# First loads and first projection of a two-layer diffusion backbone: unread products, latents first, half chunks by turns

## Chip, cores and metric

The kernel runs on one NeuronCore of a Trainium2 chip. The metric is the device time of one launch, in microseconds. Three runs of the kernel before took 780.47 us in the median (778.85 to 781.42).

## What is computed

Two layers work on 512 latent tokens (x) and 256 context tokens (ctx) of 1024 channels. The change lies at the start of the first one: the modulation (`_adaln`), the norm, and the projection by `w_in`.

```python
def _rmsnorm(x, g):
    xf = x.astype(jnp.float32)
    y = xf * lax.rsqrt(jnp.mean(xf * xf, axis=-1, keepdims=True) + RMS_EPS)
    return (y * g.astype(jnp.float32)).astype(x.dtype)

def _adaln(cond, w, b):
    m = jax.nn.silu(cond) @ w + b
    return jnp.split(m, 3, axis=-1)
...
        shift, scale, gate = _adaln(c, ada_w[layer], ada_b[layer])
        shift_c, scale_c, gate_c = _adaln(c_ctx, ada_w[layer], ada_b[layer])
        h_l = _rmsnorm(x, norm_g[layer]) * (1.0 + scale[:, None]) + shift[:, None]
        h_c = _rmsnorm(cx, norm_g[layer]) * (1.0 + scale_c) + shift_c
...
    z = jnp.concatenate([h_c, h_l], axis=1) @ w_in
```

Behind that stand latent attention and a bidirectional recurrence in layer 0 (whose decay uses `softplus(-lambda)`), neighbourhood attention in layer 1, a gate on each layer's output, and a last norm.

## The kernel before

Channels lie on the 128 partitions, tokens in the columns: x is eight tiles `x0` to `x7` of 128 x 768, columns 0 to 511 the latents (LAT), 512 to 767 the context (CTX). All is float32. A product of the projection is made of three float32r ones: each operand is split into a high and a low part (`hh`, `hl` for the normed block, `w0t0h`, `w0t0l` for a weight tile), and high x high, low x high and high x low are summed in PSUM. ScalarE writes the high part, VectorE the low one.

The first stage has these steps.

- **Loads**, all from the SP queue, which issues them in program order: x (L175), the modulation weights, the weight tiles `w0t` of the projection. `load_w` (L113) issues from there. At most eight loads are under way, since each uses one of eight semaphores in turn, and the issue that reuses one waits for the landing of the load that had it.
- **Norm** (`norm0`, L356): ScalarE squares each x tile into `sq`, VectorE adds the squares into `acc0`, PE sums them over partitions (L296, `pssum`), ScalarE takes a root (`r00t`, L304), VectorE turns it into a reciprocal root (`r00r`, L305 to L309), PE transposes and spreads it (`r00b`, L322), ScalarE copies it out as `rsb0` (L323). Names with r00 belong to the latents, with r01 to the context.
- **Modulation** (`ada_mm`, L215): 32 columns of PE at a time, eight blocks of the condition against a chunk of `ada_w`; the result is copied out (`rows`, L227), transposed (`psc`, L232) and reduced into shift `as` and scale `am` of one or two blocks (L234 to L250). Blocks 0 and 1 come as half chunks of 128 columns (`ada_prep1`, `ada_go1`, tensor `ada0`), the pairs (2,3), (4,5), (6,7) as the chunks 1, 2 and 3 of 256 columns with 5, 6 and 7 for the scale; blocks 2 and 3 are chunk 1, and the names `psada_2`, `psada_4`, `psada_6` give the first block.
- **Normed block** (`h_block` by `hb(j, c)`, L338 to L341): VectorE multiplies x by scale and root, ScalarE adds the shift into `hh`, VectorE the rest into `hl`.
- **Projection** (`z_t`, L141): tiles 0 and 1 (`psx0`, `psx1`) and 8 (`psg8`): 3 tiles x 8 blocks x 3 products, each for 512 latent and 256 context columns, 144 instructions. Then `lru_x` copies psx0 and psx1 out (L537, L539), and tile 2 follows in the same PSUM tile as psx0.

The order in which the instructions of one engine stand is not that of the code: the Tile framework sets it with a scheduler, by its own estimate of durations, and each engine then works through it strictly in order. `behind(PE, ACT)` and `tc.issue_after(mark)` tie instructions behind the last one that an engine has been given. The first stage is written out by hand from L416 to L460, the call of `z_t` for tile 8; the softplus of `lambda` is L501 to L515, the loads for the next stage are `prep_n(0)` and `ropen` (L899).

Of the kernel before, what the change touches and what calls it, by code (L numbers as in the profile page):

```python
# [46 lines left out]
def build(nc, tc, A, out, dbg=None):  # L47
# [5 lines left out]
    PE, ACT, DVE = mybir.EngineType.PE, mybir.EngineType.Activation, mybir.EngineType.DVE  # L53
# [45 lines left out]

    HE = (G,)  # L100
# [73 lines left out]
    def x_load(j):  # L174
        SY.dma_start(x_tiles[j], A["xin"][j])  # L175
# [180 lines left out]
    def norm0():  # L356
        sq = {}
        for j in range(8):
            sq[j] = th(f"sq{j}")
            S.activation(sq[j], x_tiles[j], AF.Square)  # L360
            if j == 4:
                S.activation(root, sq[0][:, 0:1], AF.Sqrt)
            for w in (LAT, CTX) if j == 7 else (slice(0, NT),):
                if j:
                    V.tensor_tensor(acc0[:, w], (acc0 if j > 1 else sq[0])[:, w], sq[j][:, w], ALU.add)
                if j == 7:
                    c = w is CTX
                    n, pp = (NL, NC)[c], (zz, zz3)[c]
                    ps = pp(f"pssum{c}")
                    sq_sum(ps, acc0[:, w], n, True, True)  # L370
                    if c == 0:
                        rs_bc("r00", ps, n, rsb0[:, w], pp)
                    else:
                        norm0c = lambda: rs_bc("r01", ps, n, rsb0[:, CTX], pp)
        return norm0c
# [51 lines left out]
    norm0c()
    with behind(PE, ACT):
        wt[0] = kfun(split_raw("w0t0", raw0, (8, 128)))
        hb(0, 1)  # L430
        ada_prep(1)
        ada_go1(1)
# [71 lines left out]
    V.tensor_scalar(z, e, 2.0, None, ALU.add)  # L504
    V.reciprocal(z, z)
    V.tensor_tensor(z, z, e, ALU.mult)
    V.tensor_tensor(w, z, z, ALU.mult)
    V.tensor_scalar(q, w, 1.0 / 19, None, ALU.mult)
    for d in range(17, 1, -2):
        V.scalar_tensor_tensor(q, q, 1.0 / d, w, ALU.add, ALU.mult)  # L510
    V.scalar_tensor_tensor(q, q, 1.0, z, ALU.add, ALU.mult)
    V.tensor_scalar(nl, nl, 0.0, None, ALU.max)
    V.scalar_tensor_tensor(sp4, q, 2.0, nl, ALU.mult, ALU.add)
    V.tensor_scalar(nsp4, sp4, -4.0, None, ALU.mult)
    V.tensor_scalar(sp4, sp4, 4.0, None, ALU.mult)  # L515
# [1326 lines left out]
```

## Time and profile before

| What | Value |
|---|---|
| median of three runs | 780.47 us |
| profiled execution, its own time | 780.51 us |
| its span | 778.7 us |
| PE busy | 742.4 us (95%) |
| DVE busy | 507.5 us (65%) |
| ACT busy | 415.6 us (53%) |
| POOL busy | 163.7 us (21%) |
| DMA, mean over the span | 122 GB/s |

Busy time is the union of an engine's instructions; a busy PE is not one at its peak, as the ends of its pipelined products are modelled. The chain that ended last is the work followed back from the last instruction, at each step to what released it: 75% of it is PE, 12% DVE, 5% ACT. The first 62 us, which the change rewrites, are read from the timeline, which lists an engine's instructions with start and duration.

### The profile page before, as it was taken

How to read it: one execution, taken by the hardware profiler on the slowest of the kernel's cores; microseconds unless marked ns; L12 is line 12 of the kernel's file. 1: busy time of each engine (PE TensorE's matmuls, PEld its weight loads, DVE VectorE, ACT ScalarE, POOL GpSimd, SP SyncE). 2: the span in 40 equal slices, each digit the busy share in tenths (PEclk: the TensorE clock that was granted, in tenths of full speed). 3: DMA queues.
4: the chain of work that ended last, by engine and by line, in shares of the span. 5: the costliest groups of instructions: out<-in, count | busy, mean ns of one | idle time of the engine just before them, and what ended most of it. 6: DMA issues, size and time to landing. Idle time of an engine off the chain costs nothing.

```text
span 778.7 us, 13220 instructions
## 1 busy us (share of the span) xinstructions
PE 742.4 (95%) x4966; PEld 652.8 (84%) x4966; DVE 507.5 (65%) x1051; ACT 415.6 (53%) x811; POOL 163.7 (21%) x191
## 2 busy tenths in 40 slices
PE   2999999999999999999999999999999999999995
PEld 2678898787788877888998899888888799889995
DVE  5748499887478777753396567546653766568544
ACT  5424867964467777542245355535542645456633
POOL 0000002003153477404210022002200211021414
PEclk9999999999999999999999999999999999999998
DMA  8913403411455553257021550236124541336203
GB/s 332 407 49 109 134 28 122 162 42 28 118 157 141 177 169 126 89 172 261 28 82 46 144 163 16 91 113 190 38 99 140 174 120 55 109 102 170 82 1 109
DMA packets 33598, 95.29 MB, mean 122 GB/s; under 512 B 4608, under 2 KB 6784, under 8 KB 33536
## 3 DMA queue, kind: packets, MB, share of 16 engines
q1 hardware_dynamic: 32960, 93.93, 37.5%
q8 instruction: 39, 0.64, 0.3%
q10 hardware_dynamic: 576, 0.52, 0.2%
q14 instruction: 23, 0.19, 0.1%
HBM read 73.99 MB, written 4.19 MB: 100 GB/s over the span
## 4 chain that ended last, share of the span: by engine, by line
PE 75%; DVE 12%; ACT 5%; issue 4%; DMA 3%; POOL 1%; SPq 0%; POOLq 0%; ACTq 0%; DVEq 0%
PE psg L141 11%; PE psv L1270 8%; PE psq L141 7%; PE w0oy L1175 7%; PE pskl L141 6%; PE psx L141 4%; PE w1oy L1175 4%; PE pt L1387 3%; PE pskc L141 3%; PE psada L215 2%; PE s L1346 2%; PE s L808 2%; PE s L1347 2%; PE po L1370 2%; PE po L1371 2%
## 5 line engine op out<-in xcount | busy, mean ns | idle before, releaser
L764 POOL TENSOR_SCALAR p<-p,rc 128x512 f32<-128x512 f32 (+1 forms) x96 | 77.7, 812 | 325.8 <-DVE rc L763 309.7
L1354 ACT ACTIVATE p<-s,nm 128x512 f32<-128x512 f32 x64 | 43.8, 686 | 37.0 <-DVE nm L1352 20.6
L1390 DVE TENSOR_TENSOR ptl<-pt,pth 128x512 fp32r<-128x512 f32 x64 | 43.6, 687 | 26.7 <-ACT pth L1389 26.7
L1389 ACT ACTIVATE pth<-pt 128x512 fp32r<-128x512 f32 x64 | 37.3, 595 | 34.7 <-PE pt L1387 25.5
L1352 DVE CUSTOM_DVE_ANT_1 s<-s,bias 128x512 f32<-128x512 f32 x48 | 33.2, 696 | 16.3 <-PE s L1347 14.3
L1387 PE MATMUL pt<-ident,p 128*128 128x128 f32 x256 | 40.0, 272 | 0.0
L615 POOL TENSOR_TENSOR mix<-mix,la 128x256 f32<-128x256 f32 x4 | 3.6, 905 | 172.8 <-DVE la L609 124.8
L844 DVE TENSOR_TENSOR pt<-pt,pt 128x512 fp32r<-128x512 f32 x48 | 31.9, 681 | 11.5 <-ACT pt L843 11.4
L843 ACT ACTIVATE pt<-pt 128x512 fp32r<-128x512 f32 x48 | 27.4, 595 | 16.1 <-PE pt L881 16.0
L763 DVE RECIPROCAL rc<-rs 128x1 f32<-128x1 f32 x96 | 15.2, 158 | 31.6 <-ACT p L1354 22.2
L1346 PE MATMUL s<-k,q 128*128 128x256 f32 x128 | 34.3, 292 | 0.4 <-DMA q<-qx 0.2
L812 ACT ACTIVATE p<-s,nm 128x768 f32<-128x768 f32 x32 | 28.8, 901 | 10.7 <-DVE nm L810 10.4
L1387 PEld LDWEIGHTS pt<-ident,p 128*128 128x128 f32 x256 | 31.1, 140 | 4.0 <-issue 0.4
L810 DVE TENSOR_REDUCE nm<-s 128x1 f32<-128x768 f32 x32 | 30.4, 951 | 4.6 <-PE s L808 4.1
L1347 PE MATMUL s<-k,q 128*128 128x256 f32 x128 | 33.3, 284 | 0.0
L1370 PE MATMUL po<-pth,v 128*128 128x256 f32 (+1 forms) x96 | 31.6, 335 | 0.0
L1371 PE MATMUL po<-ptl,v 128*128 128x256 f32 (+1 forms) x96 | 29.6, 324 | 0.0
L881 PE MATMUL pt<-ident,p 128*128 128x128 f32 x192 | 28.7, 273 | 0.0
L862 PE MATMUL po<-pt,v 128*128 128x256 f32 x96 | 26.1, 296 | 1.7 <-DVE pt L844 1.6
L861 PE MATMUL po<-pt,v 128*128 128x256 f32 x96 | 26.6, 294 | 0.4 <-DVE rcc L763 0.4
L1346 PEld LDWEIGHTS s<-k,q 128*128 128x128 f32 x128 | 24.3, 190 | 3.0 <-issue 1.4
L1200 ACT ACTIVATE sq<-xr 128x512 f32<-128x512 f32 (+1 forms) x16 | 8.2, 522 | 33.1 <-DVE xr L1181 27.1
(966 smaller groups left out, 2636.8 us busy)
## 6 DMA issues: line engine op xcount, KB each, us to landing
ada_0r<-ada SPq DMA_DIRECT2D x22, 512.0 KB, 5.0
ada_4r<-ada SPq DMA_DIRECT2D x22, 512.0 KB, 5.4
q<-qx SPq DMA_DIRECT2D x32, 256.0 KB, 5.0
bias<-bias SPq DMA_DIRECT2D x16, 256.0 KB, 2.7
x<-xin SPq DMA_DIRECT2D x8, 384.0 KB, 6.3
xr<-xin SPq DMA_DIRECT2D x8, 384.0 KB, 7.0
x1d<-xr SPq DMA_DIRECT2D x8, 256.0 KB, 5.2
x<-x1d SPq DMA_DIRECT2D x8, 256.0 KB, 4.2
```

The costliest lines, as they stand in the source:

```text
L141: P.matmul(ps, a(k), b[k][:, c], start=(k == 0 and i == 0), stop=(k == nk - 1 and i == 2),)
L764: G.tensor_scalar(p, p, rc, 0.5, ALU.mult, ALU.mult)
L1175: P.matmul(ps, a, b[k][:, c], start=(n == m == 0 and ps is dst[0][0] and not second), stop=(n == 7 and m == 2), skip_group_check=True,)
L1270: P.matmul(ps, tok(a[k], t), b[:, k % 4], start=(k == 0 and i == 0), stop=(k == 7 and i == 2))
L1346: P.matmul(s[:, :256], lhs, kap, start=(i == 0), stop=False, skip_group_check=True)
L1347: P.matmul(s[:, 256:], lhs, k2[:, CTX], start=False, stop=(i == 1), skip_group_check=True)
L1354: S.activation(p, s, AF.Exp, bias=nm, scale=-1.0, accum_out=rsum)
L1370: P.matmul(dst, vv, h, start=first, stop=False, skip_group_check=True)
L1371: P.matmul(dst, vv, l, start=False, stop=last, skip_group_check=True)
L1387: P.transpose(ps[:, 128 * j : 128 * j + 128], p1[hd, b][:, 128 * c : 128 * c + 128], ident)
L1389: S.activation(h, ps, AF.Copy)
L1390: V.tensor_tensor(l, ps, f(h), ALU.subtract)
```

## The change

It does six things. Forty products of a filled tile `junk` by itself go to PE at the start, into a PSUM tile that nobody reads. x is loaded in two parts, first the eight latent halves, then, behind the first modulation and weight loads, the eight context halves. The norm runs once for the latents and once for the context. Blocks 0 to 3 are modulated by half chunks, loaded by turns with the weight tiles 0, 1 and 8. The projection is written block by block over the three tiles (`xk`), the latents of blocks 0 to 3 before their context. Softplus is tied behind VectorE's last instruction of the stage, `w0n0` and `ropen` behind its last load.

```diff
+    WARM = 40
...
+    G.memset(junk[:, :512], 1.0)
...
+    idle = pa.tile([128, 512], F32, tag="a", name="idle")
+    for _ in range(WARM):
+        P.matmul(idle, junk[:, :128], junk[:, :512], start=True, stop=True)
...
-    def x_load(j):
-        SY.dma_start(x_tiles[j], A["xin"][j])
+    def x_load(j, c):
+        w = (LAT, CTX)[c]
+        SY.dma_start(x_tiles[j][:, w], A["xin"][j][:, w])
...
+    def norm0(c):
+
+        n, w = (NL, NC)[c], (LAT, CTX)[c]
         for j in range(8):
...
+            sq = sqc[:, j] if c else th(f"sq{j}")[:, :NL]
+            S.activation(sq, x_tiles[j][:, w], AF.Square)
+            if j == 0:
+                prev = sq
+            else:
+                V.tensor_tensor(acc0[:, w], prev if j == 1 else acc0[:, w], sq, ALU.add)
+            if j == 0 and c == 0:
+                S.activation(root, sq[:, 0:1], AF.Sqrt)
+        ps = (zz, paa)[c](f"pssum{c}")
+        sq_sum(ps, acc0[:, w], n, True, True)
+        bc(f"r0{c}", rs(f"r0{c}", ps, n), n, rsb0[:, w], (zz, paa)[c])
...
+    def xk(c, js):
+
+        w = (LAT, CTX)[c]
+        for j in js:
+            for ps, ft in FIRST:
+                wh, wl = wt[ft]
+                for i, (a, b) in enumerate(((wh, hh), (wl, hh), (wh, hl))):
+                    P.matmul(
+                        ps[:, w], a(j), b[j][:, w], start=(j == 0 and i == 0), stop=(j == 7 and i == 2)
+                    )
+
     for j in range(8):
...
+        x_load(j, 0)
+    for j, ft in ((0, 0), (1, 1)):
+        ada_prep1(j)
+        load0t(ft)
+    for j in range(8):
+        x_load(j, 1)
+    ada_prep1(2)
+    load0t(8)
+    ada_prep1(3)
+    norm0(0)
+    with behind(DVE):
+        split0t(0)
...
+    ada_go1(1)
     hb(1, 0)
...
+    with behind(DVE):
+        split0t(1)
+    norm0(1)
+    for j in range(2):
+        hb(j, 1)
...
+    ada_go1(2)
+    hb(2, 0)
+    with behind(DVE):
+        split0t(8)
+    xk(0, [0, 1, 2])
+    ada_go1(3)
+    hb(3, 0)
     ada_prep(2)
...
     ada_prep(6)
...
+    xk(0, [3])
+    for j in range(2, 4):
+        hb(j, 1)
+    xk(1, [0, 1, 2, 3])
     ada_prep(3)
...
     ada_prep(7)
...
+    for p in (2, 3):
+        ada_go(p)
+        for j in (2 * p, 2 * p + 1):
+            for c in range(2):
+                hb(j, c)
+        for j in (2 * p, 2 * p + 1):
+            for c in range(2):
+                xk(c, [j])
...
+    with tc.issue_after(h_mark):
+        V.tensor_scalar(z, e, 2.0, None, ALU.add)
...
+    with tc.issue_after(load_mark):
+        prep_n(0)
+        SY.dma_start(ropen, A["ropen"])
```

What the scheduler makes of it is seen at three places. **ACT, from the last square to the first block**, before:

```order
L360 ACTIVATE sq7_158<-x7_102 128x768
L304 ACTIVATE r00t_168<-pssumFalse_161,eps_104 128x4
L304 ACTIVATE r01t_238<-pssumTrue_182,eps_104 128x2
L227 ACTIVATE rows0_0_224<-psada0_0_207 128x128
L323 ACTIVATE rsb0_122<-r00b_175 128x512
L323 ACTIVATE rsb0_122<-r01b_245 128x256
L121 ACTIVATE w0t0h_249<-w0t0r_201 128x1024
L340 ACTIVATE hh0_185<-x0_95,as0_116 128x512
```

and now (`w0t0h`, `w0t1h` are the high parts of the weight tiles, `rows0_0` the modulation of block 0 copied out of PSUM):

```order
L369 ACTIVATE sq7_227<-x7_144 128x512
L123 ACTIVATE w0t0h_250<-w0t0r_180 128x1024
L311 ACTIVATE r00t_237<-pssum0_230,eps_146 128x4
L234 ACTIVATE rows0_0_287<-psada0_0_270 128x128
L330 ACTIVATE rsb0_164<-r00b_244 128x512
L234 ACTIVATE rows0_1_316<-psada0_1_299 128x128
L123 ACTIVATE w0t1h_328<-w0t1r_186 128x1024
L347 ACTIVATE hh0_254<-x0_137,as0_158 128x512
```

The splits of two weight tiles now stand ahead of the root and of hh0; the context's root has gone from here.

**PE, around the first products of the projection**, before:

```order
L322 MATMUL r01b_245<-ident_67,r01r_236 128x128 x2
L232 MATMUL psc0_0_226<-ident_67,rows0_0_224 128x128
L215 MATMUL psada0_1_260<-ada010r_203,c34_109 32x128 x8
L215 MATMUL psada0_1_260<-ada011r_205,c34_109 32x128 x8
L141 MATMUL psx0_441<-hh0_185,w0t0h_249 128x512
L141 MATMUL psx0_441<-hh0_185,w0t0h_249 128x256
L232 MATMUL psc0_1_279<-ident_67,rows0_1_277 128x128
L215 MATMUL psada0_2_300<-ada0_1_0r_256,c34_109 32x256 x4
L215 MATMUL psada0_2_300<-ada0_1_4r_258,c34_109 32x256 x4
L215 MATMUL psada0_2_300<-ada0_5_0r_292,c34_109 32x256 x4
L141 MATMUL psx0_441<-hl0_193,w0t0h_249 128x512
```

and now, from the last product of block 1 on:

```order
L434 MATMUL psx1_370<-hl1_263,w0t1h_328 128x512
L303 MATMUL pssum1_347<-ones_154,acc0_165 128x2 x2
L434 MATMUL psg8_371<-hh0_254,w0t8h_401 128x512
L329 MATMUL r01b_359<-ident_67,r01r_350 128x128 x2
L222 MATMUL psada0_2_372<-ada020r_196,c34_151 32x128 x8
L222 MATMUL psada0_2_372<-ada021r_198,c34_151 32x128 x8
L239 MATMUL psc0_2_391<-ident_67,rows0_2_389 128x128
L222 MATMUL psada0_3_432<-ada030r_202,c34_151 32x128 x8
L222 MATMUL psada0_3_432<-ada031r_204,c34_151 32x128 x8
L434 MATMUL psx0_369<-hh2_256,w0t0h_250 128x512
```

Between the latents of block 1 and those of block 2 now stand the sum over the context, a product of tile 8, the spreading of the context's root, and two blocks of modulation. Before, a chunk for two blocks stood there, with products of blocks 0 and 1 between and behind its parts.

**DVE, between the first latents and the context's sum**, now (`acc0` is the sum of the squares):

```order
L348 SCALAR_TENSOR_TENSOR hl0_262<-x0_137,as0_158,hh0_254 128x512
L373 TENSOR_TENSOR acc0_165<-sqc_166 128x256
L373 TENSOR_TENSOR acc0_165<-acc0_165,sqc_166 128x256 x2
L348 SCALAR_TENSOR_TENSOR hl1_263<-x1_138,as0_158,hh1_255 128x512
L127 TENSOR_TENSOR w0t1l_330<-w0t1r_186,w0t1h_328 128x1024
L373 TENSOR_TENSOR acc0_165<-acc0_165,sqc_166 128x256 x4
L312 TENSOR_SCALAR r01m_351<-pssum1_347 128x2
L313 RECIPROCAL r01r_350<-r01t_352 128x2
```

The context's sums, which were made before the first root, now alternate with the low parts of blocks 0 and 1 and of tile 1.

## Rows read from the trace of the kernel before

**Rows 1.** Waits of PE, 14 to 62 us: us in total, times, longest.

```profile
PE psx L141 <- ACT hh L340: 0.9, 2, 0.5
```

**Rows 2.** Windows: length, busy us of PE, PEld, DVE, ACT, POOL, PEclk, DMA share, GB/s.

```profile
20.00:40.00 20.00, 19.50 (x152) 12.11 (x154) 14.69 (x32) 9.46 (x16) 0.00 (x0) 1.00 1.03 408
```

**Rows 3.** Timeline of the DMA queue, loads in the first 30 us: start, us.

```profile
12.09 0.33 SPq L115 DMA_DIRECT2D ada_4r<-ada  x1
...
13.06 0.33 SPq L115 DMA_DIRECT2D ada_0r<-ada  x1
...
14.34 0.33 SPq L115 DMA_DIRECT2D ada_4r<-ada  x1
...
27.20 0.33 SPq L115 DMA_DIRECT2D ada_4r<-ada  x1
...
27.62 1.24 SPq L115 DMA_DIRECT2D ada_0r<-ada  x1
...
28.96 0.38 SPq L115 DMA_DIRECT2D ada_4r<-ada  x1
```

**Rows 4.** Timeline of POOL, its last fill but one.

```profile
0.91 0.33 POOL L188 MEMSET c<- 128x272 f32 x1
```

**Rows 5.** Timeline of PE: start, us, line, tiles, shapes, count.

```profile
19.13 1.12 PE L322 MATMUL r00b<-ident,r00r 128*128 128x128 f32 x4
...
20.47 0.42 PE L232 MATMUL psc<-ident,rows 128*128 128x128 f32 x1
...
23.23 1.01 PE L141 MATMUL psx<-hh,w0t0h 128*128 128x512 f32 x2 [0.48 <-ACT hh L340]
...
24.04 0.42 PE L232 MATMUL psc<-ident,rows 128*128 128x128 f32 x1
...
27.48 0.52 PE L141 MATMUL psx<-hh,w0t0l 128*128 128x512 f32 x2
...
27.93 0.64 PE L215 MATMUL psada<-ada_4r,c 128*32 128x256 f32 x8
...
28.49 0.62 PE L141 MATMUL psx<-hh,w0t0h 128*128 128x512 f32 x2
...
42.15 0.51 PE L141 MATMUL psx<-hh,w0t1l 128*128 128x512 f32 x2
...
42.50 0.28 PE L141 MATMUL psg<-hl,w0t8h 128*128 128x256 f32 x1
...
44.03 0.38 PE L232 MATMUL psc<-ident,rows 128*128 128x128 f32 x2
...
59.96 0.58 PE L141 MATMUL psx<-hh,w0t2h 128*128 128x512 f32 x2
```

**Rows 6.** Timeline of ACT, the first root, row scale and split.

```profile
17.44 0.26 ACT L304 ACTIVATE r00t<-pssumFalse,eps 128x4 f32<-128x4 f32 x1 [3.53 <-PE pssumFalse L296]
...
20.29 0.60 ACT L323 ACTIVATE rsb<-r00b 128x512 f32<-128x512 f32 x1 [0.74 <-PE r00b L322]
...
21.04 1.06 ACT L121 ACTIVATE w0t0h<-w0t0r 128x1024 fp32r<-128x1024 f32 x1
```

**Rows 7.** Timeline of DVE: softplus, r00r, x0, w0t0's low part, lx0.

```profile
4.49 1.37 DVE L510 SCALAR_TENSOR_TENSOR sp<-sp,sp 128x8 f32<-128x8 f32 x7
...
18.41 0.16 DVE L309 SCALAR_TENSOR_TENSOR r00r<-r00t,r00r 128x4 f32<-128x4 f32 x1
...
21.67 1.15 DVE L338 SCALAR_TENSOR_TENSOR x<-x,am,rsb 128x512 f32<-128x512 f32 x2
...
22.74 1.22 DVE L125 TENSOR_TENSOR w0t0l<-w0t0r,w0t0h 128x1024 fp32r<-128x1024 f32 x1
...
58.73 0.42 DVE L537 COPY lx<-psx 128x256 f32<-128x256 f32 x1 [4.46 <-PE psx L141]
```

**Rows 8.** Windows at the end of the span, columns as in rows 2.

```profile
769.00:771.00 2.00, 0.78 (x6) 0.61 (x5) 0.56 (x3) 0.68 (x2) 1.25 (x2) 1.00 0.52 179
...
771.00:773.00 2.00, 0.66 (x2) 0.29 (x2) 0.63 (x5) 0.38 (x1) 0.08 (x1) 0.50 0.19 66
```

More of the change, by code (lines that the diff above doesn't have):

```diff
@@ L52, in build @@
     V, S, P, G, SY = nc.vector, nc.scalar, nc.tensor, nc.gpsimd, nc.sync
-    PE, ACT, DVE = mybir.EngineType.PE, mybir.EngineType.Activation, mybir.EngineType.DVE
+    PE, ACT, DVE, SP = (getattr(mybir.EngineType, e) for e in ("PE", "Activation", "DVE", "SP"))
     def f(ap):
@@ L351, in build @@
     acc0 = px.tile([128, NT], F32, name="acc0")
+    sqc = px.tile([128, 8, NC], F32, name="sqc")
     root = cst.tile([128, 1], F32, name="root")
-    def norm0():
-        sq = {}
+    def norm0(c):
+        n, w = (NL, NC)[c], (LAT, CTX)[c]
         for j in range(8):
[L359 to L375, printed above, removed]
+            sq = sqc[:, j] if c else th(f"sq{j}")[:, :NL]
[9 more added lines that the diff above has]
+        bc(f"r0{c}", rs(f"r0{c}", ps, n), n, rsb0[:, w], (zz, paa)[c])
     wt = {}
@@ L414, in go, with load0t, split0t @@
         next(going[key], None)
-    psx = []
-    for j in range(8):
-        x_load(j)
-    ada_prep1(0)
-    norm0c = norm0()
+    raw = {}
+    def load0t(ft):
+        raw[ft] = load_w(f"w0t{ft}", A["w0t"][ft], (8, 128))
+    def split0t(ft):
+        wt[ft] = kfun(split_raw(f"w0t{ft}", raw[ft], (8, 128)))
+    def xk(c, js):
[7 more added lines that the diff above has]
+                    )
@@ L421, in build @@
+    for j in range(8):
+        x_load(j, 0)
[10 more added lines that the diff above has]
+        split0t(0)
     hh = [th(f"hh{j}", F32R) for j in range(8)]
     hl = [th(f"hl{j}", F32R) for j in range(8)]
-    raw0 = load_w("w0t0", A["w0t"][0], (8, 128))
-    ada_prep1(1)
     ada_go1(0)
     hb(0, 0)
[L427 to L432, printed above, removed]
@@ L433, in build @@
-    hb(1, 0)
-    hb(1, 1)
-    ada_prep(5)
+    ada_go1(1)
+    hb(1, 0)
+    with behind(DVE):
[3 more added lines that the diff above has]
+        hb(j, 1)
+    psx = [zz("psx0"), zz("psx1")]
+    psg8 = zz3("psg8")
+    FIRST = ((psx[0], 0), (psx[1], 1), (psg8, 8))
+    ada_go1(2)
[5 more added lines that the diff above has]
+    hb(3, 0)
     ada_prep(2)
-    ada_go(1)
     ada_prep(6)
-    hb(2, 0)
-    hb(2, 1)
+    xk(0, [3])
@@ L461, in build @@
+    h_mark = next(i for i in reversed(nc.cur_bb.bb.instructions) if i.engine == DVE)
+    load_mark = next(i for i in reversed(nc.cur_bb.bb.instructions) if i.engine == SP)
+    wt.clear()
     for j in range(8):
@@ L503, in build @@
     S.activation(e, e, AF.Exp)
[L504 to L515, printed above, removed]
+    with tc.issue_after(h_mark):
+        V.tensor_scalar(z, e, 2.0, None, ALU.add)
+        V.reciprocal(z, z)
+        V.tensor_tensor(z, z, e, ALU.mult)
+        V.tensor_tensor(w, z, z, ALU.mult)
+        V.tensor_scalar(q, w, 1.0 / 19, None, ALU.mult)
+        for d in range(17, 1, -2):
+            V.scalar_tensor_tensor(q, q, 1.0 / d, w, ALU.add, ALU.mult)
+        V.scalar_tensor_tensor(q, q, 1.0, z, ALU.add, ALU.mult)
+        V.tensor_scalar(nl, nl, 0.0, None, ALU.max)
+        V.scalar_tensor_tensor(sp4, q, 2.0, nl, ALU.mult, ALU.add)
+        V.tensor_scalar(nsp4, sp4, -4.0, None, ALU.mult)
+        V.tensor_scalar(sp4, sp4, 4.0, None, ALU.mult)
     dump("sp4", sp4)
```

22 lines of the change are left out of this document (1 added, 21 removed).

## Prediction

> **What bounds the kernel now.** I read the waits of TensorE first, then its timeline beside those of ScalarE, VectorE and the DMA queue, all for the first 62 us, since the change touches nothing behind them: the orders of the engines are otherwise the same, but for some twenty rows in the middle of PE and two or three of DVE that change places. PE waits only 0.9 us in all between its first product and 62 us [rows 1], so the stage looks like one bound by PE. That holds from 23.23 us on, when the first product of the projection starts; before that PE lacks data. Loads are the other limit: from 20 to 40 us the DMA engines are busy all the time, at 408 GB/s [rows 2]. The place to which I count is the start of the next projection, psx of tile 2, at 59.96 us [rows 5]. What moves it moves everything behind, because all later work hangs on these three tiles and PE goes on almost without a break.
>
> The column of the granted clock reads 1.00 in that stretch too [rows 2], but the products do not: the first 768 columns (512 and 256) take 0.81 us, from 23.23 to 24.04, and the same at 42.15 take 0.35 [rows 5]. At 27.48 they take 0.45, and the rows group behind it 0.56. So I go by durations: half speed (1.2 GHz) up to about 27.0, full (2.4 GHz) after 3.8 us of products. [...]
>
> **Loads.** The eighth issue behind a load waits for its landing, so x7 of before has landed at 13.06; 384 KB pass in 0.97 us, 512 KB in 1.28 [rows 3]. The only load with rows of 1 KB, ropen (128 KB), lies in the 1.76 us between 27.20 and 28.96, beside one of 512 KB: 0.48 at most, 0.42 by the gap to 27.62 [rows 3]. I take 0.42 for a ctx half and 0.70 for a lat half of x (256 KB, rows of 2 KB), between 0.64 by bytes alone and 0.76 as two ropen at the gap less what the longer row spares. Eight lat halves then end 8 x 0.27 = 2.2 us earlier, and w0t0, third behind them, lands at 13.06 - 2.2 + 3 x 1.28 = 14.7. Three more of 512 KB, eight ctx halves (3.4) and three (ada020, ada021, w0t8) put w0t8 at 25.8. The chunks 2 and 3 end by 38.6; none of the rest is late. By bytes alone it would be w0t0 at 14.2, w0t8 at 24.5. The Trainium skill (DMA: Bandwidth & Descriptors, Specifications) puts the smallest transfer that runs at line rate at 512 bytes, and by it the shorter rows would cost nothing and my sum would be 0.5 us smaller.
>
> **Unread products.** Forty of 512 columns start when POOL has filled junk, at some 1.3 us, behind the fills that now end at 1.24 [rows 4]. At two thirds of 0.81 for the first 3.8 us and of 0.35 after, they end near 12.7. The first sum is ready then, but its root is not taken before 15.85 (below), so they cost nothing; were that cover gone, each would cost 0.23.
>
> **First half block.** On ScalarE the split of w0t0 now stands ahead of the root r00t. It waits for the load: 14.7 + 1.06 [rows 6] + 0.1 = 15.85. From r00t to the end of r00r took 17.44 to 18.57 [rows 6, 7]; three tiny instructions slipped in, 0.1 each, make it 1.4: 17.3. The transposes r00b stand behind eight products of psada0_1, which wait for psc of block 0, and start near 17.6; with 1.12 [rows 5] and rsb 0.60 [rows 6] it is 19.3. ScalarE then has rows0_1 and the split of w0t1 (1.06) ahead of hh0: 20.85. With hh0 at two thirds of a pair, 0.73, the first product starts at 21.5 instead of 23.23, at half clock, which the trickle of products from 12.7 on cannot have kept up (16 small ones per half chunk, as little as at the end of the span).
>
> **From there to hh2, the term that decides.** In the order, r01b and the whole of block 2 stand behind one product of psg8 and behind the sum over the context, and that sum is built on VectorE between other things: hl0 0.77, three acc of 256 columns (0.38 as the third of a pair [rows 7], and 0.07 to the next that needs it) 1.35, hl1 0.77, the low part of w0t1 1.22 [rows 7], four acc 1.8. That is 5.9 us: 27.4. PE's twelve products (0.54 each for 3.8 us, then 0.23) are through by 26.5, before that sum. Then sum products 0.6, root and rsqrt 1.1, r01b 0.5 (half of r00b), rsb and x0 of the context 0.8, hh0 and hh1 of the context 0.8, rows0_2 0.25: 31.4. From psc to the first product behind it took 20.47 to 23.23, 2.76 us [rows 5], here for block 2: 34.2. w0t8 (25.8 + 1.06 = 26.9) is in time for its product, the half chunks too. So PE, with only 13 of its 144 projection products behind it, has stood idle for most of 6 us.
>
> **From hh2 to the end.** Up to psc of chunk 2 PE has 23 products of 512 columns and 36 of 256, by the full pair's 0.35 [rows 5] 5.4 + 4.2 us, four groups of psada at 0.56 [rows 5] and psc 0.4: 12.3. From that psc on, the work is what it was: 44.03 to 59.96, 15.93 us [rows 5], the wait for hh4 in it. 34.2 + 12.3 + 15.9 = 62.4, against 59.96: 2.4 us. The clock fell again while PE stood, so the first 3.8 us run at half speed and lose 1.9: 64.3. The sum is **+4.4 us**.
>
> **What costs nothing.** Softplus (18 small instructions at 0.2 [rows 7], 3.6 us) moves from under the loads to behind hl7. VectorE is idle there for 4.46 us until psx0 is done [rows 7]; without that cover it would delay the copy of psx0 and so psx of tile 2 by up to 3.6. The w0n0 and ropen loads move behind the chunks, some 2 us later than now, for work behind psx of tile 2. The eight additional squares and adds lie beside PE's waits, and are in the chain above where they are not.
>
> The profiled execution took 780.51 us with its span of 778.7, 0.04 above the median of 780.47. So 780.5 + 4.4 = **784.9 us**. A measurement here can tell about 0.3% (2.3 us) from no change.
>
> **Rivals.**
> (1) The clock stays full from the unread products on. Half of the 1.12 of r00b and a half chunk's 0.5 are saved ahead of the first product, 1.2 in all, and the 1.9 behind hh2: +1.3, 781.8. With loads by bytes alone, +0.8. [...] Against it: what the engine does at 14 to 23 now, the same small products, left it at half speed. Chance 0.25.
> (2) Each pause of PE brings half clock back, and 12 products with pauses in them never lift it: the sum products, r01b and two half chunks then take 1.3 us more ahead of hh2. That is +5.7, 786.2. The Trainium skill (TensorE: Matmul & The Clock Gate, HAM oscillation) tells of bursts of matmuls parted by waits for loads, each of which starts throttled; the fall at 771 agrees, and no row of before shows a rise broken off. Chance 0.16.
> (3) It gets faster, because PE, waiting 0.9 us in all [rows 1], is what paces the stage: an earlier first product, 20.3 at full clock, brings everything forward by 2.9 and spares the 1.9 lost between 23.23 and 27: 775.7. This needs PE fed without a break. It decides at hh2: with 12.3 + 15.9 behind it, the product of hh2 must come before 31.7 for no loss and before 29.4 for a gain that shows. Against it: with loads by bytes alone the product of w0t8 cannot come before 24.5 + 1.06, and behind that stand r01b, a half chunk, and 2.76 us. Chance 0.08.
> (4) The unread products do not do what they say: the clock stays down under them (forty at 0.54, two thirds of 0.81, to 22.9) and the first sum waits for them in PE's queue. r00t comes near 25, not 15.95: some 793. Against it, 3.8 us of products lifted the clock at 27. Chance 0.06.
>
> **Numbers.** The forecast has 0.45. Its own bounds are -1.0 (loads by bytes, a shorter step in the VectorE chain) and +1.2. Range 780.0 to 787.0: it takes in the forecast, (1) with its lower bound, and (2), and leaves out (3) and (4). Slower by over 0.3%: 0.45 + 0.16 + 0.06 and the upper edge of (1), 0.03: 0.70. Faster 0.08. The same 0.22.
>
> **What would show it.** Right: psx of tile 2 starts between 63 and 66 us, hh2's first product at 33 to 36, PE idle or in half chunks between 27 and 34, r00t behind the split of w0t0. The pair of 768 columns (or 512 alone, 0.5 against 0.23) at half speed at 21 and again at 35. VectorE's lx directly behind psx0, not behind softplus. Wrong: hh2 before 31.7, or full speed at 21 and at 35; and if psx of tile 2 is late by 4 us but the end is not, later work had slack that I don't see.

## The result and the profile after

The changed kernel takes 788.12 us (median of 4 runs, 785.01 to 789.13) against 779.78 for the kernel before (4 runs beside it). The ratio is 1.0101, 95% interval 1.0082 to 1.0119: slower, as forecast, but by 8 us instead of 4.4, and outside the range. The profiled execution took 788.36 us with a span of 786.5.

On the page of the changed kernel TensorE is busier in all, by 14.5 us, of which the unread products, from 1.46 to 12.34, are 10.9. The clock's row shows one slice of 20 us at half:

```profile
span 786.5 us, 13395 instructions
...
PE 756.9 (96%) x5038; PEld 659.0 (84%) x5038; DVE 510.4 (65%) x1061; ACT 416.1 (53%) x820; POOL 164.1 (21%) x192
...
PEclk9599999999999999999999999999999999999998
```

The windows of that stretch (columns as in [rows 2]) say how long it lasts. TensorE works 6.2 to 7.1 us of each 8, at 0.50 of full speed from 16 to 40 us; 0.51 in the third row is the last tenths behind the rise:

```profile
16.00:24.00 8.00, 6.16 (x43) 3.69 (x44) 5.74 (x20) 4.87 (x13) 0.00 (x0) 0.50 0.91 306
24.00:32.00 8.00, 6.89 (x31) 4.28 (x34) 4.71 (x13) 2.58 (x6) 0.00 (x0) 0.50 1.01 371
32.00:40.00 8.00, 7.13 (x78) 4.26 (x74) 6.72 (x18) 2.46 (x6) 0.00 (x0) 0.51 0.89 319
40.00:48.00 8.00, 8.00 (x55) 5.34 (x44) 2.66 (x5) 2.29 (x4) 0.00 (x0) 1.00 0.76 280
```

The timeline of PE in the changed kernel, answering to [rows 5]: start, duration, line, tiles, and in brackets the idle time ahead and who ended it.

```profile
1.46 10.88 PE L161 MATMUL idle<-junk 128*128 128x512 bf16 x40 [1.46 <-POOL eps L187]
12.43 0.64 PE L222 MATMUL psada<-ada000r,c 128*32 128x128 f32 x16
...
16.31 0.47 PE L239 MATMUL psc<-ident,rows 128*128 128x128 f32 x1 [1.68 <-ACT rows L234]
...
21.87 0.79 PE L434 MATMUL psx<-hh,w0t0h 128*128 128x512 f32 x1 [1.08 <-ACT hh L347]
22.46 0.63 PE L434 MATMUL psx<-hh,w0t0l 128*128 128x512 f32 x1
...
28.04 0.63 PE L434 MATMUL psx<-hl,w0t1h 128*128 128x512 f32 x1
28.46 0.85 PE L303 MATMUL pssum<-ones,acc 128*128 128x2 f32 x4
...
30.61 0.66 PE L329 MATMUL r01b<-ident,r01r 128*128 128x128 f32 x2 [0.66 <-DVE r01r L316]
31.20 1.08 PE L222 MATMUL psada<-ada020r,c 128*32 128x128 f32 x16
...
33.59 0.48 PE L239 MATMUL psc<-ident,rows 128*128 128x128 f32 x1 [0.46 <-ACT rows L234]
...
36.34 0.80 PE L434 MATMUL psx<-hh,w0t0h 128*128 128x512 f32 x1 [0.41 <-ACT hh L347]
...
40.59 0.50 PE L434 MATMUL psx<-hl,w0t0h 128*128 128x512 f32 x1
...
50.90 0.38 PE L239 MATMUL psc<-ident,rows 128*128 128x128 f32 x2
...
67.18 0.58 PE L143 MATMUL psx<-hh,w0t2h 128*128 128x512 f32 x2 [0.56 <-DVE lx L570]
```

The row at 12.43 is the first real product; 36.34 is the first of block 2; 50.90 are the columns of chunk 2; 67.18 is the start of tile 2, the place to which the prediction counts. It was at 59.96 [rows 5], so 7.2 of the 7.9 us between the two profiled executions are lost ahead of it.

**An account for the first stretch.** The time to tile 2 can be split into three parts that add up: the start of TensorE's first real product, the time behind it in which no real product ran (unread products count as waiting), and the rest, in which TensorE works on real products. That work is nearly the same in all kernels here, about 40 us at full clock, so what the last part has above 40 is, in the main, half clock. Worked out from the rows of PE's timeline:

| kernel | start | waits | busy | tile 2 at | profiled run | behind tile 2 | median, runs | ratio to before, 95% |
|---|---|---|---|---|---|---|---|---|
| before | 14.46 | 1.04 | 44.46 | 59.96 | 780.51 | 720.6 | 780.47, 3 | |
| changed | 12.43 | 6.20 | 48.55 | 67.18 | 788.36 | 721.2 | 788.12, 4 | 1.0101 (1.0082, 1.0119) |
| e1 no unread products | 11.67 | 8.16 | 47.91 | 67.74 | 792.86 | 725.1 | 792.13, 4 | 1.0150 (1.0125, 1.0176) |
| e2 before, with them | 14.37 | 2.64 | 41.05 | 58.06 | 784.52 | 726.5 | 783.05, 10 | 1.0030 (1.0012, 1.0047) |
| e3 27 fillers | 12.98 | 11.91 | 44.02 | 68.91 | 792.23 | 723.3 | 790.26, 4 | 1.0123 (1.0092, 1.0154) |
| e4 before, with fillers | 15.32 | 3.67 | 40.35 | 59.34 | 783.15 | 723.8 | 782.32, 10 | 1.0025 (1.0014, 1.0035) |
| e5 11 fillers, same order | 12.44 | 9.08 | 44.62 | 66.14 | 787.66 | 721.5 | 787.11, 4 | 1.0086 (1.0068, 1.0104) |
| e6 x whole | 15.06 | 3.97 | 41.90 | 60.93 | 783.93 | 723.0 | 783.25, 5 | 1.0043 (1.0029, 1.0057) |
| e7 context behind | 12.27 | 6.59 | 43.08 | 61.94 | 783.40 | 721.5 | 783.54, 4 | 1.0044 (1.0029, 1.0059) |
| e8 chunk 1 whole | 12.70 | 8.69 | 46.54 | 67.93 | 794.22 | 726.3 | 793.67, 4 | 1.0172 (1.0157, 1.0187) |
| e9 13 fillers | 12.57 | 8.99 | 41.49 | 63.05 | 783.79 | 720.7 | 784.75, 4 | 1.0065 (1.0046, 1.0083) |
| e10 e7 with 6 fillers | 12.55 | 6.65 | 39.60 | 58.80 | 779.04 | 720.2 | 779.67, 10 | 1.0001 (0.9992, 1.0011) |
| e11 no ties | 12.63 | 6.12 | 46.71 | 65.46 | 787.34 | 721.9 | 786.00, 4 | 1.0081 (1.0066, 1.0096) |

So the change starts real work 2.0 us earlier, then waits 5.2 us more and works 4.1 us longer on the same products: +7.2. The four runs of the changed kernel fit a loss by the clock: ordered by time, 789.13, 788.36, 787.89 and 785.01 us, their mean granted clocks are 0.978, 0.981, 0.981 and 0.986. The two questions for the experiments are what the half clock is worth, and what the waits come from. The column "behind tile 2" turned out to matter too, and comes last.

### The profile page after: what moved, and what is told of

It is laid out like the page before. It is cut to its first block, busy times and chain, and to the rows that moved or that the text cites. A ratio compares the mean times of both kernels' runs of the same rounds, so it can differ in the third digit from the quotient of the medians.

```text
span 786.5 us, 13395 instructions
## 1 busy us (share of the span) xinstructions
PE 756.9 (96%) x5038; PEld 659.0 (84%) x5038; DVE 510.4 (65%) x1061; ACT 416.1 (53%) x820; POOL 164.1 (21%) x192
## 4 chain that ended last, share of the span: by engine, by line
PE 73%; DVE 11%; ACT 5%; DMA 4%; issue 4%; POOL 2%; SPq 1%; POOLq 0%; ACTq 0%; DVEq 0%
PE psg L143 9%; PE psv L1302 8%; PE w0oy L1207 7%; PE psq L143 6%; PE pskl L143 6%; PE w1oy L1207 4%; PE pt L1419 3%; PE pskc L143 3%; PE psada L222 2%; PE psx L434 2%; PE s L1378 2%; PE s L839 2%; PE s L1379 2%; PE po L1402 2%; PE po L1403 2%
## 5 line engine op out<-in xcount | busy, mean ns | idle before, releaser
L1422 DVE TENSOR_TENSOR ptl<-pt,pth 128x512 fp32r<-128x512 f32 x64 | 43.7, 688 | 26.5 <-ACT pth L1421 26.5
L1384 DVE CUSTOM_DVE_ANT_1 s<-s,bias 128x512 f32<-128x512 f32 x48 | 33.2, 696 | 16.4 <-PE s L1379 14.5
L874 ACT ACTIVATE pt<-pt 128x512 fp32r<-128x512 f32 x48 | 27.4, 595 | 16.1 <-PE pt L912 16.0
L1378 PE MATMUL s<-k,q 128*128 128x256 f32 x128 | 34.2, 291 | 0.8 <-DMA q<-qx 0.8
L789 DVE TENSOR_TENSOR cb<-po,cb 64x512 f32<-64x512 f32 (+1 forms) x25 | 16.6, 666 | 13.5 <-ACT cb L788 13.3
```

The source lines that it names most:

```text
L1378: P.matmul(s[:, :256], lhs, kap, start=(i == 0), stop=False, skip_group_check=True)
L1422: V.tensor_tensor(l, ps, f(h), ALU.subtract)
```

## Experiments

**e1 and e2: the unread products alone.** e1 has WARM = 0 in the changed kernel:

```
-    WARM = 40
+    WARM = 0
```

> The changed kernel without its 40 unread products; nothing else differs. Theory (the clock falls at 15.9 us with or without them, and the order of blocks 2 and 3 and the half clock behind it cost the time): only the first modulation products and the latents' sum (12.4 to 14.6 us) run at half clock instead of full, the first product of block 0 starts within 0.6 us of 21.87, block 2's within 1.0 us of 36.34, and the time is 787.5 to 789.5, within 1.5 us of the changed kernel. Rival A (the unread products are what costs, by power or by blocking TensorE): under 786. Rival B (they bring what the forecast counted on): over 790.

The first product of block 0 started at 21.81, block 2's at 36.84, tile 2 0.56 us later than in the changed kernel, but the time is 792.13. Of the 4.5 us between the two profiled executions, 3.9 lie behind tile 2. The expectation of 787.5 to 789.5 failed, and by time this is rival B's case (over 790); up to tile 2 the theory's numbers held. The half microsecond is a balance and not the price of the unread products alone: without them real work starts 0.76 us earlier, waits grow by 1.96 and busy time falls by 0.64. The edit also moved the queues. The product of tile 8 now stands ahead of the context's sum, and ScalarE makes hh of block 1 at 24.24 instead of 22.94, which brings a wait that the changed kernel does not have. The timeline of PE in e1:

```profile
25.02 0.80 PE L434 MATMUL psx<-hh,w0t0h 128*128 128x512 f32 x1 [1.85 <-ACT hh L347]
```

Its clock was full from 20.0 to 23.4 us and, behind the same twelve products, from 30.2 to 33.6. The windows of e1 show the second rise:

```profile
23.40:30.20 6.80, 4.91 (x13) 3.48 (x13) 3.72 (x7) 1.78 (x2) 0.00 (x0) 0.50 1.02 414
30.20:33.60 3.40, 1.65 (x36) 1.15 (x36) 1.60 (x7) 1.13 (x4) 0.00 (x0) 1.00 0.49 190
```

e2 adds them to the kernel before:

```
+    G.memset(junk[:, :512], 1.0)
...
+    idle = pa.tile([128, 512], F32, tag="a", name="idle")
+    for _ in range(40):
+        P.matmul(idle, junk[:, :128], junk[:, :512], start=True, stop=True)
```

> The kernel before with the 40 unread products at its start; nothing else differs. Theory (they only hold the clock while they run): they end near 12.4, TensorE stands until its first real product at 14.5, the clock falls again behind 15 us, the first product of block 0 starts at 22.5 to 23.3, and the time is within 1 us of the kernel before. Rival A (TensorE is busy from 14.46 on without a longer gap, so the full clock survives): first product of block 0 at 22.5 or earlier, the granted clock full from 6 us on, and 2 to 5 us gained. Rival B (they cost): over 1 us slower.

Here they bring 1.9 us at tile 2: the clock fell for one spell only (0.79 in the window of 16 to 24 us), busy went from 44.46 to 41.05, and 1.6 us of that came back as waits. TensorE's order is that of the kernel before up to 23.8 us; behind that some thirteen instructions change places, so a part of the gain can be the order's. The clock did fall behind the unread products, at 16.45, as the theory has it, but it was back at 19.9, where the kernel before has it from 26.9 on. So "they only hold the clock while they run" is not the whole of it: what stands behind them counts too. In e2 TensorE waits 0.26 us between 14.4 and 20.7, in the changed kernel 1.68 us at 14.6, and there the clock is down from 16 to 40. The first product of block 0 came at 21.94. The time of e2 is nevertheless 2.8 us longer than before, which by time is rival B's case ("they cost"); it is lost behind tile 2.

**e3 and e4: fillers in the gaps.** Both put further unread products into gaps, tied behind the real product ahead of them; e3 into the changed kernel, up to 33 us. The expectation counts 21 of them; the numbers in the edit add up to 27 (21 in the list, 6 behind the context's sum):

```
+    HOLD = {(0, 0, 0): 6, (0, 1, 0): 2, (0, 1, 1): 5, (0, 2, 0): 2, (0, 2, 1): 6}
+    def hold(n):
+        if n:
+            with behind(PE):
+                unread(n)
...
         sq_sum(ps, acc0[:, w], n, True, True)
+        hold((0, 6)[c])
```

> The changed kernel with 21 more unread products in TensorE's gaps between 14 and 34 us (6, 2, 5 behind the first modulation columns, 6 behind the context sum, 2 and 6 around block 2's columns); what is computed is the same. Theory (of the 7.7 us some 4 are the half clock of 15.9 to 39.8, and the pauses cause it): the granted clock stays full to 26 us at least, the first 12 products run 0.23 us apart, block 2's first product starts 1 to 2 us earlier than 36.34 and the columns of chunk 2 come 12 to 13 us behind it instead of 14.56; 783.5 to 786. Rival A (the order alone costs the time, the clock is no loss since the chain over ACT and DVE sets block 2): within 1 us of the changed kernel. Rival B (the fillers delay real work): slower than the changed kernel by over 1 us.

> The kernel before with 48 unread products at its start and 12 more in TensorE's gaps up to 23 us (4 and 2 behind the two sums, 2 and 4 behind the first two modulation columns); the context sum's tile lies in another pool. Theory (half clock to 27 us costs the kernel before TensorE time that nothing else hides): the clock is full from 6 us on, the 16 modulation products of a column take 0.64 us instead of 1.08, the first product of block 0 starts at 22.3 to 23.2, and 1.5 to 5 us are gained: 775 to 779. Rival (loads and the chain over ACT and DVE set the stretch to 40 us): within 0.7 us of the kernel before. Rival (fillers in front of real work): slower by over 1 us.

In e3 the clock was full to 58 us and block 2's first product came at 33.87, 2.5 us earlier. But the compiler's scheduler, which lays out TensorE's queue by estimated times, put the columns of chunk 3 behind nearly all other products, and block 6 waited for them. The timeline of PE in e3:

```profile
39.71 0.38 PE L251 MATMUL psc<-ident,rows 128*128 128x128 f32 x2
...
56.28 0.44 PE L251 MATMUL psc<-ident,rows 128*128 128x128 f32 x2 [0.55 <-ACT rows L246]
59.01 0.80 PE L448 MATMUL psx<-hh,w0t0h 128*128 128x512 f32 x1 [2.29 <-ACT hh L360]
```

The wait of 2.29 and the half clock that begins in it (0.80 for a product that takes 0.50) hide the gain. In time e3 is 2.1 us longer than the changed kernel, by the numbers rival B (the fillers delay real work), here by way of the order: the wait behind chunk 3. As a test of the clock it is inconclusive. e4 moved the order as well (the first modulation products now stood behind the fillers of the sums), reached full clock throughout (busy 40.35), and gained 0.6 us at tile 2, below the expected 1.5 to 5. In time it lost 2 us, the case of the second rival, whose mechanism shows in a start of real work 0.86 us later (15.32).

**e5: fillers, with TensorE's order unchanged.** The counts were chosen so that every real instruction of TensorE up to tile 2 keeps its place.

```
+    HOLD = {(0, 0, 0): 6, (0, 1, 0): 1, (0, 1, 1): 4}
```

> The changed kernel with 11 more unread products in three gaps of TensorE before its first real product (6 behind the first modulation columns, 1 and 4 around the second's); unlike the kernel with 21 fillers, TensorE's real instructions up to tile 2 keep exactly the order of the changed kernel. Up to the first product of tile 2 that kernel's time is start 12.43 + waits 6.20 + busy 48.55 = 67.18 us. Theory (half clock and waits cost about as much each; a faster TensorE turns part of its gain into waits for ScalarE and VectorE): the clock is full to 24 us at least, busy falls to 43 to 46.5, waits rise to 7 to 10, tile 2 starts at 64.0 to 66.5. Rival A (half clock is nearly all of it): tile 2 at 63 or earlier. Rival B (chain alone): tile 2 at 66.7 or later. The time of the runs: 785 to 788.

The windows of e5:

```profile
24.00:28.00 4.00, 2.21 (x10) 1.56 (x10) 1.79 (x6) 1.21 (x2) 0.00 (x0) 1.00 1.02 418
28.00:32.00 4.00, 2.57 (x40) 1.44 (x44) 2.50 (x10) 1.45 (x4) 0.00 (x0) 0.74 1.01 408
32.00:36.00 4.00, 3.60 (x36) 2.58 (x32) 3.50 (x9) 1.28 (x3) 0.00 (x0) 0.50 0.92 304
36.00:40.00 4.00, 4.00 (x28) 1.50 (x26) 3.28 (x10) 1.12 (x2) 0.00 (x0) 0.50 0.98 359
```

With the clock full to 30 us, TensorE is busy only 2.2 of 4 us between 24 and 28: it waits for the low part of w0t1 (0.63), for the context's sum (0.57), for the split of w0t8 (1.04) and for the context's root (0.59). There the clock falls, for 10 us. Busy is 3.9 us shorter than in the changed kernel, waits 2.9 longer, tile 2 at 66.14, within the expected 64.0 to 66.5. Block 2's first product came at 34.15, almost where the forecast had it (34.2), but by two errors that cancel: the sum's products came at 26.19 instead of 27.4, and from there to psc of block 2 passed 5.2 us instead of 4.0. What was gained up to there was half lost again in the dense products behind it, which now ran at half clock.

**e9: fillers up to block 2.**

```
+    HOLD = {(0, 0, 0): 5, (0, 1, 0): 1, (0, 1, 1): 2, (0, 2, 1): 3}
...
+        hold((0, 2)[c])
```

> The changed kernel with 13 more unread products: 5, 1 and 2 in the gaps around the first two modulation columns, 2 behind the context's sum and 3 behind block 2's columns, so up to block 2's first product; TensorE's real instructions keep the changed kernel's order but for seven moved by a few places between 28 and 42 us. The run with 11 fillers up to 20 us kept the clock full to 30 us, had block 2's first product at 34.2 and tile 2 at 66.14. Theory (with the clock full to tile 2 the remaining loss is the order's, near what the forecast had for it): clock full to 60 us, busy near 41, waits 8 to 10.5, tile 2 at 62.0 to 64.0, time 782.5 to 785.5. Rival A (waits take all of it): tile 2 at 65 or later. Rival B (the waits of 25 to 33 us bring half clock in spite of the fillers): half clock within 28 to 40 us and tile 2 at 65.5 to 66.5.

The clock stayed full but for one spell of 3.4 us, from 30.2 to 33.6, which the expectation did not have. It takes a little under half of each of the first two windows:

```profile
28.00:32.00 4.00, 2.87 (x39) 1.85 (x39) 2.60 (x9) 1.45 (x4) 0.00 (x0) 0.77 1.04 412
32.00:36.00 4.00, 4.00 (x45) 2.53 (x48) 3.25 (x6) 1.40 (x3) 0.00 (x0) 0.80 0.85 310
36.00:40.00 4.00, 4.00 (x40) 2.31 (x32) 2.77 (x8) 1.12 (x2) 0.00 (x0) 1.00 0.94 316
```

Tile 2 starts at 63.05, 4.1 us before that of the changed kernel (theory: 62 to 64), and the time is 784.75, 3.4 us less. Seven rows of TensorE's order differ, so this is close to a test of the clock alone, not quite one. It leaves 3.1 us against the kernel before, of which the spell that is left accounts for 1.7 at most (an estimate: half of 3.4).

**e6, e7 and e8: which part of the order.** e6 loads x whole again and takes both sums of squares in front of block 0:

```
-    for j in range(8):
-        x_load(j, 0)
+    for j in range(8):
+        x_load(j)
...
-    for j in range(8):
-        x_load(j, 1)
...
     norm0(0)
+    norm0(1)
```

> The changed kernel with x loaded whole, as before the change, and with both sums of squares (latents and context) in front of block 0; half chunks, products by turns, unread products and ties stay. Theory (the context's sum, put behind the latents, is what stops TensorE between 26 and 36 us): TensorE starts later (14.5 to 15.5 instead of 12.43) but has the waits of 0.67, 0.46 and 0.41 us at 30 to 36 us no more, block 2's first product starts before 33, tile 2 at 60 to 64. Rival A (half chunks in place of chunk 1 are what costs): tile 2 at 66 or later in spite of it. Time by the theory 781 to 786, by rival A over 787.

e7 keeps the latents first, and moves all of the context behind them:

```
-    for j in range(8):
-        x_load(j, 1)
     ada_prep1(2)
     load0t(8)
     ada_prep1(3)
+    for j in range(8):
+        x_load(j, 1)
...
     xk(0, [3])
+    norm0(1)
-    for j in range(2, 4):
+    for j in range(4):
         hb(j, 1)
```

> The changed kernel with the context's loads, sum of squares and first products moved behind the latents' products of blocks 0 to 3 (loads behind the half chunks of block 3); all else stays. Theory (the latents alone have enough products to fill TensorE from 22 us on, if nothing of the context stands in front of block 2): block 2's first product starts at 28 to 31 us instead of 36.34, the waits from 25 to 36 us are gone, tile 2 starts at 61.5 to 64.5; 782 to 785.5. Rival A (the loads decide, and the context now comes too late): a wait of over 2 us for the context's sum between 33 and 42 us, tile 2 at 66 or later. Rival B (the scheduled clock decides): half clock to 38 us again and tile 2 at 65 to 66.

e8 undoes the half chunks of blocks 2 and 3:

```
-    ada_prep1(2)
+    ada_prep(1)
     load0t(8)
-    ada_prep1(3)
+    ada_prep(5)
...
-    ada_go1(2)
+    ada_go(1)
...
-    ada_go1(3)
```

> The changed kernel with chunk 1 whole, as before the change, in place of the half chunks of blocks 2 and 3; latents first, unread products, products by turns and ties stay. Theory (not the half chunks but the context in front costs): block 2's first product starts 35.5 to 37.5, tile 2 at 65.5 to 68, time within 1.5 us of the changed kernel (786.6 to 789.6). Rival (the four half chunks, one after the other through ScalarE and VectorE, cost): tile 2 at 65 or earlier and over 2 us gained.

e6 and e7 take opposite ways and end alike: 783.25 and 783.54, some 4.7 us less than the changed kernel, tile 2 at 60.93 and 61.94. In e6 TensorE starts 2.6 us later, waits 2.2 us less and is at full clock but for two short spells; in e7 block 2's first product comes at 29.71 instead of 36.34. Half chunks and products by turns stay in both. e8, without half chunks, is no better at tile 2 (67.93); it has the context in front and in addition a wait of 2.29 us for chunk 3 at 58, the one that e3 showed. Its block 2 began at 38.51 and its time is 793.67, both outside what was expected. Its profiled run is 5.9 us longer than that of the changed kernel, of which 5.1 lie behind tile 2. So the place of the context's sum is what stops TensorE, as the theory has it: with the half chunks kept, moving it either way gives 5 to 6 us at tile 2. What the half chunks cost by themselves e8 does not settle. Without the wait of 2.29 its tile 2 would lie some 1.5 us ahead of the changed kernel's (an estimate, 67.93 less 2.29 against 67.18). The order of the products block by block over the three tiles was undone in no run.

The waits alone do not show this. e7 waits as long as the changed kernel (6.59 against 6.20), and not all waits ahead of 36 us are gone, as its theory had it: 1.02 and 1.40 us are left there, both for hh. But TensorE is busy for 7.33 of the 8 us from 16 to 24, where the changed kernel has 6.16, the clock rises at 25.8 instead of 39.8, and busy time falls by 5.5 us. The windows of e7:

```profile
16.00:24.00 8.00, 7.33 (x59) 4.65 (x60) 5.95 (x19) 3.25 (x6) 0.00 (x0) 0.50 1.02 406
24.00:32.00 8.00, 6.85 (x67) 4.33 (x66) 4.38 (x10) 4.29 (x12) 0.00 (x0) 0.89 0.83 266
```

**e10: both together.** e7 with 5 and 1 fillers, real instructions of TensorE in the order of e7:

```
+    HOLD = {(0, 0, 0): 5, (0, 1, 0): 1}
```

> The kernel with the context behind the latents of blocks 0 to 3, with 6 unread products more (5 and 1 in the gaps behind the first two modulation products); the order of TensorE's real instructions is that kernel's. It had start 12.27 + waits 6.62 + busy 43.05 = 61.94. Theory (half clock from 15.9 to 26 us is worth its 2.5 us of busy time, of which waits for ScalarE and VectorE take back about half): clock full to tile 2, busy 40.3 to 41, waits 7.5 to 9, tile 2 at 60.0 to 61.3, time 781 to 783.3. Rival (loads and chain set it): tile 2 within 0.4 of 61.94, time unchanged against 783.54.

This is the clean test of the clock: TensorE's and ScalarE's orders are those of e7, and on VectorE three instructions change places, ahead of the first product of block 0. The windows show the clock full throughout:

```profile
16.00:24.00 8.00, 6.92 (x83) 4.34 (x83) 6.34 (x16) 4.42 (x7) 0.00 (x0) 1.00 1.03 401
24.00:32.00 8.00, 5.66 (x50) 3.48 (x48) 6.47 (x18) 4.06 (x11) 0.00 (x0) 1.00 0.95 320
```

Busy falls by 3.5 us and the waits stay (6.65 against 6.59). The theory had half of the gain coming back as waits, and tile 2 at 60.0 to 61.3; none of it came back, and tile 2 is at 58.80. The timeline of PE in e10, with block 2 at 26.58 and the two longest waits that are left, for hh of block 3 and for the context's root:

```profile
26.58 0.50 PE L447 MATMUL psx<-hh,w0t0h 128*128 128x512 f32 x1 [0.80 <-ACT hh L360]
...
32.06 0.50 PE L447 MATMUL psx<-hh,w0t0h 128*128 128x512 f32 x1 [1.44 <-ACT hh L360]
...
36.03 0.40 PE L342 MATMUL r01b<-ident,r01r 128*128 128x128 f32 x2 [1.30 <-DVE r01r L329]
...
58.80 0.59 PE L143 MATMUL psx<-hh,w0t2h 128*128 128x512 f32 x2 [0.55 <-DVE nsp L555]
```

Tile 2 starts 1.2 us ahead of the kernel before. The time, 779.67 (10 runs) against 779.92, ratio 1.0001 (0.9992 to 1.0011), is the same as before. It is the best of the variants, and no faster than what there was; why the 1.2 us do not show in the medians is open.

**e11: without the ties.**

```
-    with tc.issue_after(h_mark):
+    with ExitStack():
...
-    with tc.issue_after(load_mark):
+    with ExitStack():
```

> The changed kernel without the two ties: softplus and the loads behind it are ordered by the scheduler again. Forecast and theory (the ties cost nothing, since VectorE waits for TensorE where softplus now stands): tile 2 within 0.5 us of 67.18, time within 1.5 us of the changed kernel, 786.6 to 789.6. Rival (softplus late on VectorE makes lx and tile 2 late): tile 2 at 66.6 or earlier and over 1.5 us gained.

Tile 2 came at 65.46 and the time is 2.1 us less, which by the numbers is the rival's case; the forecast failed. The rival's mechanism is not there: tile 2 waits some 0.56 us for lx in both, and by the account the gain is busy time (46.71 against 48.55), since the clock rose at about 37 us instead of 39.8. In the changed kernel VectorE still waits behind softplus, so softplus delays nothing:

```profile
64.44 0.17 DVE L546 TENSOR_SCALAR sp<-sp 128x8 f32<-128x8 f32 x1
65.94 0.42 DVE L568 COPY lx<-psx 128x256 f32<-128x256 f32 x1 [1.34 <-PE psx L434]
```

Two of TensorE's products also change places. Whether the clock rises earlier because of the edit or by chance, one profile each does not tell; the runs of the two overlap (785.90 to 787.34 against 785.01 to 789.13).

**Behind tile 2.** The kernels are nearly alike there, yet the profiled executions differ from 720 to 726 us. e1, e2 and e8 are the long ones, and in all three TensorE waits near 600 us for one load that is on time elsewhere. The timelines of the DMA queue and of PE in e2:

```profile
588.33 1.55 SPq L116 DMA_DIRECT2D ada_4r<-ada  x1
```

```profile
598.65 0.35 PE L1350 MATMUL s<-k,q 128*128 128x256 f32 x1 [2.56 <-DMA q<-qx]
```

and in the kernel before:

```profile
588.50 0.42 SPq L115 DMA_DIRECT2D ada_4r<-ada  x1
```

```profile
596.43 0.36 PE L1346 MATMUL s<-k,q 128*128 128x256 f32 x1 [0.17 <-DMA q<-qx]
```

The clock falls right behind that wait in e2, as the window shows (0.57; it is at half from 600.1 to 603.5), and the two together cost 4 us (2.4 of longer wait and half of 3.4):

```profile
600.00:604.00 4.00, 4.00 (x13) 3.18 (x12) 2.58 (x9) 2.72 (x6) 1.38 (x2) 0.57 0.08 30
```
In e2 and e8 the issue of the load ahead of q took 1.55 and 1.33 us instead of 0.42; in e1 it did not, and q was 2.6 us late all the same. Why it is late in these three stays open. e2, e3, e4 and e6 show another half-clock spell of 3.4 us between 306 and 321 us, behind a wait of 1.9 to 2.1 us for ScalarE (tile `p`); the kernel before, e1, e7 and e8 have a wait of 1.85 to 2.05 there and no spell, so that wait alone does not decide it. In e2 the later q and the two spells come to 2.4 + 1.7 + 1.7 us (an estimate, with half of each spell as its cost), of the 5.9 that it is longer behind tile 2 than the kernel before. So its gain of 1.9 us did not reach the end of its profiled run, and small differences in these times should be read at tile 2 first.

## Why the prediction was wrong

Direction and place were right; the size was not. Step by step:

- **Loads.** w0t0 is split at 14.88 (14.7 plus a little was forecast). w0t8 landed at 27.4, not 25.8. The windows of the changed kernel show where that comes from:

```profile
17.00:19.00 2.00, 2.00 (x26) 1.25 (x22) 1.54 (x6) 0.12 (x1) 0.00 (x0) 0.50 1.07 356
19.00:22.00 3.00, 1.47 (x18) 0.70 (x10) 1.82 (x6) 2.50 (x5) 0.00 (x0) 0.50 0.71 217
22.00:28.00 6.00, 5.56 (x11) 3.26 (x12) 5.48 (x11) 3.40 (x10) 0.00 (x0) 0.50 1.01 342
```

From 17 to 19 us, when nearly all that moves is ctx halves, it is 356 GB/s, so 0.37 us for a half; the forecast's 0.42 was no worse than that. By the Trainium skill (DMA: Bandwidth & Descriptors, Specifications) these rows would run at line rate; the trace has 356 GB/s with the engines busy throughout, against 408 in [rows 2], so they come near it and do not reach it. The time was lost behind them: from 19 to 22 the DMA engines were busy for only 0.71, and from 22 to 28 loads of 512 KB moved at 342 GB/s. Why is open. It cost nothing at tile 2 that the trace shows, since the split of w0t8 was over before its product's turn came, behind the context's sum.
- **Unread products.** Through at 12.34 (12.7), and they did lift the clock, from 5.7 us on. Rival 4 is out.
- **First half block.** r00t at 15.84 (15.85), r00b at 17.73 (17.6), the first product at 21.87 (21.5): right to 0.4 us.
- **To hh2.** VectorE had the context's sum at 28.04 (27.4; the multiply of x1 stands ahead of hl0 and was not counted). TensorE came to it at 28.46 without an idle moment, since the last of the twelve products started at 28.04. From there to psc of block 2 passed 5.13 us instead of 4.0 (e3, at full clock, has 4.27), and block 2's first product came at 36.34 instead of 34.2. The order and the chain were as described: sum, root, r01b, the half chunk, 2.75 us from psc to the product (2.76).
- **The step that failed** is the clock in that stretch: "PE's twelve products (0.54 each for 3.8 us, then 0.23) are through by 26.5". They lifted nothing. From 22.46 to 28.04 they ran 0.43 us apart, or waited, so that TensorE's own products and not VectorE's sum set the start of the chain, 1.1 us behind the forecast; and the clock rose only at 39.8, behind block 2's first products and chunk 2's. So the sum, r01b and the half chunks ran at half speed within the chain. Of the 2.9 us by which tile 2 came later than the forecast's 64.3, 2.1 had gone by hh2. Behind it the forecast was near: 14.56 us to psc of chunk 2 against 12.3 + 1.9, and from that psc 16.28 against 15.93, with the wait for lx in it.
- **Why it failed.** I took from the trace before that a run of products soon lifts the clock. That trace showed it for products without a break; here they had pauses of 0.34 to 0.66 us and a stretch of small ones. That the pauses alone are the reason is argued and not shown: in e1 the clock was up again at 30.2 behind the same products, with a pause of 1.85 us among them. Rival 2 named what happened, with 0.16. Its price was 1.5 us too small at tile 2. Of that 0.8 lies ahead of hh2, since it let the sum's products begin at 27.4 and left out that the twelve products themselves take longer at half clock; 0.4 and 0.35 us lie behind hh2. What is cited with it (the Trainium skill, TensorE: Matmul & The Clock Gate, HAM oscillation) is a case of long waits for loads between bursts of matmuls. The trace after is not that case: it has 0.50 over 24 us in which TensorE was busy for 20, and its longest wait from 16.4 us on is 1.08 us, for ScalarE.
- **The size of the two terms.** For full clock throughout the forecast's rival 1 had +1.3 at tile 2, and so 3.1 us for half clock. e9, with one spell of half clock left, has +3.1 for the order and 4.1 for the clock. If that spell costs all of its 1.7 us, it is 1.4 and 5.8. So by e9 the clock's term was too small either way; whether the order's was too is not told. The range was too narrow because its upper end lay only 0.8 us above rival 2 at its price.
- **Rival 3**, faster through an earlier first product, put its point at hh2 before 29.4 to 31.7. e7 and e10 put it lower: with hh2 at 29.71 and half clock until 26, tile 2 is 2 us late; at 26.58 and full clock it is 1.2 us early. In both the context's work comes behind hh2, and 32.2 us pass from there to tile 2, where the forecast had 28.2.
- **The ties.** In the changed kernel softplus delays nothing, as forecast. That the ties cost nothing at all is not shown: without them the time was 2.1 us less, and whether that is the ties or the clock's chance stays open.

## What to carry to other kernels

Before counting on a warm clock, look at whether the engine has work without pauses behind the warm-up: the same forty products brought 1.9 us at tile 2 where the queue behind them was nearly full, and half a microsecond where it had gaps (in both pairs of kernels the order differs a little as well). When a reordering puts a chain through other engines in front of ready work in TensorE's queue, price it twice, once as waits and once as half clock on everything until the queue is dense again; the account of start, waits and busy time up to a fixed product shows both. Fillers, and even the removal of some products, can move the scheduler's order (e1, e2, e3, e4), so compare the order before comparing times.

## What the runs showed that was not expected

- Faster products can simply become longer waits: in e5 busy fell 3.9 us and waits rose 2.9, while in e10 busy fell 3.5 and waits did not rise. The two have different orders; why the one pays and the other does not was not tested.
- A single late load deep in the kernel (2.4 to 2.6 us for q near 600 us) had a spell of half clock behind it in each of the three runs that show it, and the pair costs about 4 us. In three of the eleven experiments it outweighed what the first 60 us had to show.
- Halves of x with rows of 1 KB moved at 356 GB/s, where the 512 KB loads from 20 to 40 us of the kernel before have 408 [rows 2].
